# Convolution's and attention's output projections as seven block products, with the gated sum taken by DMA in DRAM

## The chip, the cores and the metric

One core of a Trainium2 chip runs the kernel in one launch. The metric is the device time of that launch in microseconds. Shown are three runs of the kernel before and one profiled execution, from which all rows come. In the profile PE is TensorE's matmuls and PEld its weight loads, DVE is VectorE, ACT ScalarE, POOL GpSimd and SP SyncE, which here only issues DMAs.

## The reference

The layer takes x of 1024 tokens by 1024 channels, all in float32. Three branches are computed from h = RMSNorm(x), each with an output projection of 1024 x 1024 and a gate per element:

```python
o = rms_norm(o, subln_g) * jnp.asarray(1.0 - lam_init, o.dtype)
y_attn = o.reshape(B, S, DIFF_WIDTH) @ w_attn_o
y_conv = short_gated_conv(conv_in, conv_w) @ w_conv_o
y_mem = memory_attention(q_m, mem_n, w_mem_kv, mq_norm_g, mk_norm_g) @ w_mem_o
g = jax.nn.sigmoid((gate_logits + b_gate).astype(jnp.float32))
merged = g[:, :, 0] * y_attn + g[:, :, 1] * y_conv + g[:, :, 2] * y_mem
x = x + merged @ w_o
x = x + jnp.square(jax.nn.relu(rms_norm(x, norm_mlp_g) @ w_mlp_in)) @ w_mlp_out
```

## The kernel before

Every large product is taken in float32r with both operands split in two: a high half (a ScalarE cast) and a low half (a subtraction, mostly on VectorE), and three matmuls, high x high, high x low and low x high, add up in PSUM. So 1024 channels of one 128 x 512 block are 8 x 3 = 24 matmuls of 512 columns.

There are two sets of buffers. In the old pool (tile pool and psum, lines 112 and 113) the kernel norms x, computes the memory branch and the attention heads, and fills PE's gaps with matmuls of a generator, `stream`: first convolution and gate projections (`fill_steps`), then the three output projections (`merge_steps`). What the branches gave lies in DRAM by channel: m_dram, c_dram, o_dram and the gate logits z_dram. `sum_jobs` (line 529) forms sums of MLP weight blocks DRAM to DRAM by DMAs on POOL's queue, one job in three stages of attention (line 833); they are needed since the MLP's two products are already done as seven block products instead of eight (a Winograd form of Strassen's scheme, `ORDER` at line 842).

The output projections run after the last head, PE in the order in which it is written out (`T.pin`), loads in the order in which SP is given them (`pin_load`). `prep(b)` loads and splits the whole operand of branch b into old-pool slots while the branch ahead of it ends; `branch_steps(b)` (line 571) goes over eight column blocks of 128 channels c and two halves of 512 tokens. Each has 24 matmuls. VectorE multiplies the PSUM result with the sigmoid of the gate (lines 589 and 591), POOL adds it to merged (line 592), and for the last branch POOL stores merged to mg_dram (line 594). Other engines' orders are set by a scheduler that works from priorities and its own idea of times.

Then the old pool is closed and the new one (`xp`, `bp`, line 862 on) begins. `load_m` and `load_wo` fetch merged and w_o, `wo_mm` multiplies eight token tiles, `wo_out` adds x, norms, and stores, and `up_steps` (line 1027) runs the up-projection's block products in the order of `seq1` (line 933): pairs (g, i) of column group g and product i. Products 1, 6, 7 and 4 add up in PSUM banks X, products 2, 5 and 3 in banks Z; after 1, 6 and 7 ScalarE copies X to a tile snap (line 1045), which the next product in the same X banks has to wait for. Tags give the numbers of buffers: "wraw" 4, "wop" 3, "sn" 3, "c" 7, "x" 14, "t" 4 halves.

Of the kernel before, what the change touches and what calls it, by code (L numbers as in the profile page):

```python
# [60 lines left out]
def tile_hybrid_block(ctx: ExitStack, tc: tile.TileContext, x, mem, norm_mix_g, norm_mem_g, w_in, b_gate,  # L61
# [483 lines left out]


    mg_dram = dram.tile([KT, P, S], F32, name="mg_dram")
    merged = [None] * KT

    srcs = {2: (w_mem_o, m_dram), 1: (w_conv_o, c_dram), 0: (w_attn_o, o_dram)}  # L550
    ready = {}
# [19 lines left out]
    def branch_steps(b):  # L571
        w_src = srcs[b][0]
        w, z = ready.pop(b)
        for c in range(KT):
            gt = rowt("gt")
            load(gt, z_dram[b, c])
            A.activation(gt, gt, AF.Sigmoid, bias=bg[:, b * KT + c:b * KT + c + 1])
            wn = load_w(w_src[:, (c + 1) * P:(c + 2) * P], P, "wh") if c + 1 < KT else None
            if b == 2:
                merged[c] = slot("merged", F32, tag="m")  # L580
            if c == KT - 1:
                if b:
# [18 lines left out]

    def load_head(h):
# [205 lines left out]
    for s in range(ns):  # L808
# [67 lines left out]
        return xp.tile([P, 1024 // n, n], F32, tag="wraw", bufs=4, name=name)  # L876

    def blk(name, tag):
        return xp.tile([P, 2, 512], F32, tag=tag, bufs={"sn": 3, "c": 7}[tag], name=name)

    def half_blk(name):
        return xp.tile([P, 512], F32, tag="t", bufs=4, name=name)

# [7 lines left out]
    tq = {t: half_blk("t2") for t in range(4, NT)}  # L891
    xr = {}

    def load_m(hf, kk):
# [23 lines left out]
    def wo_out(t, ps):  # L918
# [16 lines left out]
    for g in range(2, NG):  # L935
        seq1 += [(g, 6), (g, 5), (g, 7)]
        for i, last in ((1, 4), (2, 3)):
            if g < NG - 1:
                seq1.append((g + 1, i))
            seq1.append((g, last))  # L940
    R1, W1 = {}, {}

    def load1(n):
        if n < len(seq1):
            g, i = seq1[n]
            r = R1[n] = raw4("w1raw", 256)
            if i in (1, 2, 4):
                h, c = {1: (0, 0), 2: (1, 0), 4: (1, 1)}[i]
                load(r, w1v[h, c, g])
            else:  # L950
                load(r, sw1[{5: 0, 7: 1, 6: 2, 3: 3}[i]].rearrange("(k p) (g n) -> g p k n", p=P, n=256)[g])

    def split1(n):
        if n < len(seq1):
            t = W1[n] = wpair("w1", 256)
            split(t, R1.pop(n), V)


    X = {}
# [59 lines left out]
    def put_u(i, g, t):  # L1019
        G.dma_start(u_dram[i, g], t)  # L1020

    ps1 = {}

    def up(n):
        run(up_steps(n))

    def up_steps(n):

        g, i = seq1[n]
        key = "X" if i in (1, 6, 7, 4) else "Z"  # L1030
        if i in (1, 2, 5):
            ps1[g, key] = banks(key)
        ps = ps1[g, key]
        w = W1.pop(n)
        for j in range(2):
            for k in range(4):
                for q, (a, b) in enumerate(((0, 0), (0, 1), (1, 0))):
                    T.matmul(ps[:, j, :], lhsT=w[:, a, k, j * P:(j + 1) * P], rhs=X[i][b][:, k, :],
                             start=i in (1, 2, 5) and k == 0 and q == 0, stop=k == 3 and q == 2,
                             skip_group_check=True)  # L1040
                    if (12 * j + 3 * k + q) % 8 == 7 and k + j + q < 6:
                        yield
        if i in (1, 6, 7):
            s = B[g, "s", i] = blk("snap", "sn")
            A.copy(out=s, in_=ps)
        if i == 2:
            out1(g, "c11", ps, B.pop((g, "s", 1)))
            put_u(1, g, B[g, "c11"])
        if i == 7:
            out1(g, "c22", ps1[g, "Z"], B.pop((g, "s", 7)), -1)  # L1050
            put_u(4, g, B[g, "c22"])
        if i == 4:
            out1(g, "c21", ps, sign=-1)
# [1 line left out]
        if i == 3:  # L1055
            out1(g, "c12", ps, B.pop((g, "s", 6)))
            c11, c12, c21, c22 = (B.pop((g, c)) for c in ("c11", "c12", "c21", "c22"))

            sub(V, c22, c22, c12)
            sub(V, c12, c11, c12)  # L1060
            V.scalar_tensor_tensor(out=c11, in0=c22, scalar=-1.0, in1=c11, op0=ALU.mult, op1=ALU.subtract)
            V.scalar_tensor_tensor(out=c21, in0=c21, scalar=-1.0, in1=c11, op0=ALU.mult, op1=ALU.subtract)
            for k, t in ((5, c22), (7, c12), (6, c11), (3, c21)):
                put_u(k, g, t)

    load_m(0, 0)
    load_wo(0)
# [24 lines left out]
    for t in range(4, NT):  # L1092
        ps = banks("XZ"[t % 2])
        wo_mm(ps, t, range(KT), (0,))
        first_half(t - 4)
        wo_mm(ps, t, range(KT), (1,))
        wo_out(t, ps)
        second_sums(t)
        load1(t - 4)
        if t >= 6:  # L1100
            split1(t - 6)
    alloc_x(6, 5, 7, 4, 3)
    for n in range(len(seq1)):
        load1(n + 4)
        split1(n + 2)
        if n < 4:
            parts = second_half(4 + n)
            for _ in up_steps(n):
                run(parts, 1)
            run(parts)  # L1110
        else:
            up(n)


    w2v = w_mlp_out.rearrange("(h g j p) (d n) -> h d g p j n", h=2, j=2, p=P, d=2)
# [121 lines left out]
```

## Time and profile before

| | us |
|---|---|
| median of 3 runs | 2261.43 |
| lowest, highest | 2259.38, 2262.69 |
| profiled execution, its own time | 2260.93 |
| its span | 2259.2 |
| PE busy | 2200.5 |
| DVE, ACT, POOL busy | 1165.6, 943.8, 574.3 |

A matmul's busy time runs past the start of the next one, so the start-to-start distance is what a matmul costs in a row without gaps. A timeline row is start, busy time, engine, line, operation, out<-in, shape and, in brackets, the idle time before it and what ended that. A row of the windows is the window, its length, busy time and count of PE, PEld, DVE, ACT and POOL, PE's granted clock as a share of 2.4 GHz, the mean busy share of the 16 DMA engines and GB/s. A row of instruction groups is line, engine, operation, out<-in, shapes and count, then busy time in all, mean ns of one, and idle time before with its releasers.

### The profile page before, as it was taken

How to read it: one execution, taken by the hardware profiler on the slowest of the kernel's cores; microseconds unless marked ns; L12 is line 12 of the kernel's file. 1: busy time of each engine (PE TensorE's matmuls, PEld its weight loads, DVE VectorE, ACT ScalarE, POOL GpSimd, SP SyncE). 2: the span in 40 equal slices, each digit the busy share in tenths (PEclk: the TensorE clock that was granted, in tenths of full speed). 3: DMA queues.
4: the chain of work that ended last, by engine and by line, in shares of the span. 5: the costliest groups of instructions: out<-in, count | busy, mean ns of one | idle time of the engine just before them, and what ended most of it. 6: DMA issues, size and time to landing. Idle time of an engine off the chain costs nothing.

```text
span 2259.2 us, 30413 instructions
## 1 busy us (share of the span) xinstructions
PE 2200.5 (97%) x11280; PEld 1893.7 (84%) x11280; DVE 1165.6 (52%) x2127; ACT 943.8 (42%) x2134; POOL 574.3 (25%) x813
## 2 busy tenths in 40 slices
PE   6999999999999999999999999999999999999999
PEld 6999888888888888888888888877778888788887
DVE  6755455555555555555555333324446555754442
ACT  5544445444545454454545432312333222444331
POOL 5422223232333333232323223430401010000000
PEclk9999999999999999999999999999999999999999
DMA  6412246546554575561211544544336555865571
GB/s 198 133 59 64 88 158 157 124 147 168 143 156 145 117 166 144 160 147 43 84 43 71 162 159 135 169 162 169 121 104 213 182 202 185 305 261 186 199 267 57
DMA packets 225108, 336.11 MB, mean 149 GB/s; under 512 B 17216, under 2 KB 156480, under 8 KB 221632
## 3 DMA queue, kind: packets, MB, share of 16 engines
q1 hardware_dynamic: 183760, 203.98, 27.6%
q0 software_dynamic: 24320, 104.86, 16.6%
q10 hardware_dynamic: 16880, 25.33, 3.1%
q8 instruction: 89, 1.46, 0.3%
q14 instruction: 59, 0.48, 0.1%
HBM read 267.02 MB, written 134.22 MB: 178 GB/s over the span
## 4 chain that ended last, share of the span: by engine, by line
PE 89%; DVE 4%; DMA 3%; ACT 2%; issue 2%; POOL 0%; SPq 0%; ACTq 0%; DVEq 0%; POOLq 0%
PE ps_mm L89 42%; PE X L89 16%; PE Z L89 13%; PE ps_sc L89 11%; PE ps_tr L89 3%; PE ps_tr L93 3%; DVE wlo L186 1%; PE Z L93 1%; DMA rawh<-in_w_in_dram 0%; DVE ql L666 0%; ACT qh L661 0%; DMA w2raw<-in_w_mlp_out_dram 0%; DMA mraw<-mg_dram 0%; DMA xt<-in_x_dram 0%; DVE whl L186 0%
## 5 line engine op out<-in xcount | busy, mean ns | idle before, releaser
L89 PE MATMUL ps_mm<-hT,whi 128*128 128x512 f32 x1536 | 490.8, 400 | 0.7 <-DVE vst L636 0.7
L89 PEld LDWEIGHTS ps_mm<-hT,whi 128*128 128x128 f32 x1536 | 279.7, 189 | 51.0 <-DVE vst L636 2.5
L89 PE MATMUL ps_mm<-hT,wlo 128*128 128x512 f32 x768 | 301.9, 393 | 0.0
L89 PE MATMUL ps_mm<-whh,hT 128*128 128x384 f32 x1024 | 276.7, 341 | 2.2 <-DVE inner L477 1.9
L186 POOL TENSOR_TENSOR wlo<-raw,whi 128x512 fp32r<-128x512 f32 (+2 forms) x120 | 139.1, 1164 | 214.0 <-ACT whi L204 186.5
L89 PEld LDWEIGHTS ps_mm<-whh,hT 128*128 128x128 f32 x1024 | 186.4, 188 | 7.9 <-DVE inner L477 3.7
L89 PE MATMUL X<-w,u 128*128 128x512 f32 x768 | 174.9, 389 | 1.3 <-ACT snap L1185 1.3
L89 PE MATMUL ps_mm<-whl,hT 128*128 128x384 f32 x512 | 172.0, 336 | 2.5 <-DVE whl L186 1.8
L89 PEld LDWEIGHTS X<-w,u 128*128 128x128 f32 x768 | 144.1, 188 | 31.6 <-ACT snap L1185 1.7
L89 PEld LDWEIGHTS ps_mm<-hT,wlo 128*128 128x128 f32 x768 | 144.9, 189 | 27.6
L204 ACT CAST whi<-raw 128x512 fp32r<-128x512 f32 (+2 forms) x240 | 117.8, 537 | 66.7 <-PE ps_sc L89 22.0
L638 POOL TENSOR_TENSOR sq<-qk 128x256 f32<-128x256 f32 x64 | 41.8, 654 | 382.0 <-ACT qk L633 382.0
L186 DVE TENSOR_TENSOR wlo<-raw,whi 128x512 fp32r<-128x512 f32 (+2 forms) x120 | 102.4, 857 | 68.9 <-ACT whi L204 68.2
L176 POOL TENSOR_TENSOR r<-r,mhalf 128x1 f32<-128x1 f32 (+1 forms) x186 | 133.1, 715 | 15.3
L89 PE MATMUL Z<-w,u 128*128 128x512 f32 x576 | 131.6, 389 | 1.6 <-DVE snap L854 1.6
L89 PEld LDWEIGHTS Z<-w,u 128*128 128x128 f32 x576 | 108.0, 188 | 24.7 <-DVE snap L854 2.4
L89 PE MATMUL ps_mm<-x,whi 128*128 128x512 f32 x384 | 119.1, 391 | 0.0
L89 PE MATMUL ps_sc<-x,whi 128*128 128x512 f32 x384 | 118.3, 389 | 0.0
L175 POOL TENSOR_SCALAR r<-ss 128x1 f32<-128x1 f32 (+1 forms) x186 | 37.3, 201 | 287.2 <-ACT ps_tr L732 131.4
L691 ACT ACTIVATE e<-ps_sc,negm 128x256 f32<-128x256 f32 (+7 forms) x128 | 94.1, 740 | 31.6 <-DVE negm L688 31.6
L1020 POOL DMA_DIRECT2D u_dram<-c x56 | 29.9, 535 | 300.7 <-DVE c L1016 148.9
L89 PE MATMUL ps_mm<-whi,hT 128*128 128x256 f32 x512 | 102.9, 292 | 0.0
(238 smaller groups left out, 4552.4 us busy)
## 6 DMA issues: line engine op xcount, KB each, us to landing
raw<-in_w_in_dram SPq DMA_DIRECT2D x56, 512.0 KB, 3.9
u_dram<-c POOLq DMA_DIRECT2D x56, 512.0 KB, 3.7
uraw<-u_dram SPq DMA_DIRECT2D x56, 512.0 KB, 6.3
sw<-in_w_mlp_in_dram POOLq DMA_DIRECT2D x6, 4096.0 KB, 24.6
sw<-in_w_mlp_out_dram POOLq DMA_DIRECT2D x6, 4096.0 KB, 28.6
w1raw<-sw SPq DMA_DIRECT2D x32, 512.0 KB, 3.3
w2raw<-sw SPq DMA_DIRECT2D x32, 512.0 KB, 4.5
rawh<-in_w_in_dram SPq DMA_DIRECT2D x64, 192.0 KB, 2.8
```

The source lines that it names most:

```text
L89: return cls.pin(nc.tensor.matmul(*a, **kw))
L93: return cls.pin(nc.tensor.transpose(*a, **kw))
L175: G.tensor_scalar(r, ss, 1.0 / n, EPS, op0=ALU.mult, op1=ALU.add)
L176: last_norm[0] = G.tensor_tensor(out=r, in0=r, in1=mhalf[:, 0:width], op=ALU.pow)
L186: eng.tensor_tensor(out=lo, in0=raw, in1=f(hi), op=ALU.subtract)
L204: A.copy(out=hi[:, a:b, :], in_=raw[:, k0 + a:k0 + b, :])
L638: G.tensor_tensor(out=sq, in0=qk, in1=qk, op=ALU.mult)
L691: A.activation(e[:, 0:n], sc[:, 0:n], AF.Exp, scale=-1.0, bias=negm[:, c:c + 1], accum_out=sums[:, c:c + 1])
L1020: G.dma_start(u_dram[i, g], t)
```

## The change

The memory branch stays where it was. It gates its result and stores it to mg_dram from ScalarE's queue. The other two projections leave the old pool. They become 2 x 14 block products of 24 matmuls in the new pool, ahead of w_o: two column groups of 256 and seven products, with the weights' sums formed in DRAM beforehand by 16 further jobs (1 MB each), and the operand's sums by VectorE. Each of the eight results of a branch (256 channels by 512 tokens) is gated and added to mg_dram by a DMA on POOL's queue with `accum_op=add`. The class Stage takes the place of load1, split1 and up_steps, for both the branches and the up-projection. Besides, the up-projection's last two groups get another order, and its first loads and splits are written ahead of wo_out.

```diff
+    sbr = {b: [dram.tile([512, 512], F32, name=f"sb{b}{i}") for i in range(4)] for b in (1, 0)}
...
+        todo = [([w[h * 512:(h + 1) * 512, c * 512:(c + 1) * 512] for c in range(2) for h in range(2)], sbr[n])
+                for n, w in ((1, w_conv_o), (0, w_attn_o))]
+        for (q, t, r, s), z in todo + [(a, sw1), ((b[0], b[2], b[1], b[3]), sw2)]:
...
-            if c == KT - 1:
-                if b:
-                    prep(b - 1)
...
-                if b == 2:
-                    V.tensor_tensor(out=merged[c][:, sl], in0=ps, in1=gt[:, sl], op=ALU.mult)
-                else:
-                    V.tensor_tensor(out=gt[:, sl], in0=ps, in1=gt[:, sl], op=ALU.mult)
-                    G.tensor_tensor(out=merged[c][:, sl], in0=merged[c][:, sl], in1=gt[:, sl], op=ALU.add)
-                if b == 0:
-                    G.dma_start(mg_dram[c][:, sl], merged[c][:, sl])
+                V.tensor_tensor(out=gt[:, sl], in0=ps, in1=gt[:, sl], op=ALU.mult)
+                store(mg_dram[c][:, sl], gt[:, sl])
...
-        for b in (2, 1, 0):
-            yield from branch_steps(b)
+        yield from branch_steps(2)
...
-        if s % 3 == 1:
+        if 2 <= s < 18 or s % 3 == 0:
             run(jobs, 1)
...
+    one = [(0, 1), (0, 2), (1, 1), (1, 2), (0, 6), (0, 5), (0, 7), (1, 6), (0, 4), (1, 5), (1, 7), (0, 3), (1, 4),
+           (1, 3)]
...
+    def gate(g, i):
+        b, gg = g
+        ch, th = {2: (0, 0), 7: (1, 1), 4: (1, 0), 3: (0, 1)}[i]
+        c = 4 * ch + 2 * gg
+        t = gates[g, i] = blk("gt", "t")
+        load(t, z_dram[b, c:c + 2, :, th * 512:(th + 1) * 512].rearrange("c p n -> p c n"))
+        for j in range(2):
+            A.activation(t[:, j], t[:, j], AF.Sigmoid, bias=bg[:, b * KT + c + j:b * KT + c + j + 1])
+        return c, th
+
+    def done_br(g, i, ps, s):
+        if i in (1, 6, 7):
+            t = snaps[g, i] = blk("snap", "sn")
+            A.copy(out=t, in_=ps)
+        if i in (2, 7, 4, 3):
+            c, th = gate(g, i)
+            z = gates.pop((g, i))
+            if i == 4:
+                src = ps
+            else:
+                src = snaps.pop((g, {2: 1, 7: 7, 3: 6}[i]))
+                add(V, src, s.ps[g, "Z"], src)
+
+            V.scalar_tensor_tensor(out=z, in0=src, scalar=-1.0 if i in (7, 4) else 1.0, in1=z, op0=ALU.mult,
+                                   op1=ALU.mult)
+            G.dma_start(mg_dram[c:c + 2, :, th * 512:(th + 1) * 512].rearrange("c p n -> p c n"), z,
+                        accum_op=ALU.add)
...
+    for n in range(len(seq_br)):
+        q, m = divmod(n, len(one))
+        br.load(n + 4)
+        br.split(n + 2)
+        if q == 0 and m < 4:
+            run(prep, 1)
+        if q + 1 < len(BR) and m == 4:
+            nxt = chain(first_br(BR[q + 1]), second_br(BR[q + 1]))
+        run(br.steps(n))
+        if m in (5, 6, 10, 11, 13):
+            run(nxt, 1)
...
+    g, h = NG - 2, NG - 1
+    seq1 += [(g, 6), (g, 5), (g, 7), (h, 1), (g, 4), (h, 2), (h, 6), (h, 5), (h, 7), (g, 3), (h, 4), (h, 3)]
...
+        up.load(t - 4)
+        if t >= 6:
+            up.split(t - 6)
         wo_out(t, ps)
         second_sums(t)
-        load1(t - 4)
-        if t >= 6:
-            split1(t - 6)
```

`Stage.load(n)` loads the weight block of product n (512 KB), `split(n)` makes its halves and `steps(n)` gives PE its 24 matmuls. `first_br(b)` loads four operand blocks of branch b (`block`: 256 channels by 512 tokens) and splits them for products 1 and 2 (`put_br`: one instruction on ScalarE and one on VectorE); `second_br(b)` loads twelve more, forms the sums and splits those of products 6, 5, 7, 4 and 3. Gate tiles have the tag "t", which now has two buffers.

The first place is ScalarE's order where the work goes from the old pool to the new. Before (raw tiles of merged and w_o are mraw and woraw):

```order
L577 ACTIVATE gt<-gt,bg 128x1024
L204 CAST whi<-raw 128x384 x2
L204 CAST whi<-raw 128x256
L577 ACTIVATE gt<-gt,bg 128x1024
L860 CAST mT_15527<-mraw 128x1024
L860 CAST wo_15507<-woraw 128x1024
L860 CAST wo_15508<-woraw 128x1024
```

And in the changed kernel (wraw is a product's weight block, xb1 and xb2 are operands of products 1 and 2):

```order
L579 ACTIVATE gt<-gt,bg 128x1024
L101 DMA mg_dram<-gt 128x512 x6
L851 CAST w<-wraw 128x1024 x2
L968 CAST xb1h<-raw 128x1024 x2
L851 CAST w<-wraw 128x1024
L968 CAST xb2h<-raw 128x1024 x2
L940 COPY snap<-X 128x1024
```

Six stores of the memory branch stand there now, then two weight casts, and the casts of merged and w_o have moved behind the two branches.

The second place is SP's order around the loads of merged. Before:

```order
L98 DMA gt<-z_dram 128x1024
L98 DMA raw<-in_w_attn_o_dram 128x8x128
L98 DMA gt<-z_dram 128x1024
L98 DMA mraw<-mg_dram 128x2x512
L98 DMA woraw<-in_w_o_dram 128x1024 x2
L98 DMA mraw<-mg_dram 128x2x512
```

And in the changed kernel (sb_105 is one of the four sums of the attention projection's weights):

```order
L98 DMA wraw<-in_w_attn_o_dram 128x4x256
L98 DMA gt<-z_dram 128x2x512
L98 DMA wraw<-sb_105 128x4x256
L98 DMA gt<-z_dram 128x2x512 x4
L98 DMA mraw<-mg_dram 128x2x512
L98 DMA woraw<-in_w_o_dram 128x1024 x2
L98 DMA mraw<-mg_dram 128x2x512
```

Four gate loads stand in a row ahead of the first mraw, where one stood.

The third place is PE's order near the end of the up-projection, in its last column group. Before, product 7 ends and product 4 begins in the same banks X:

```order
L89 MATMUL X<-x7h,w_18014 128x512 x2
L89 MATMUL X<-x7l,w_18014 128x512
L89 MATMUL X<-x7h,w_18014 128x512
L89 MATMUL X<-x4h,w_18043 128x512
L89 MATMUL X<-x4l,w_18043 128x512
```

In the changed kernel:

```order
L89 MATMUL X<-x7h,w 128x512 x2
L89 MATMUL X<-x7l,w 128x512
L89 MATMUL X<-x7h,w 128x512
L89 MATMUL Z<-x3h,w 128x512
L89 MATMUL Z<-x3l,w 128x512
```

The 24 matmuls of product 3 of the group before now stand between product 7 and product 4.

## Rows read from the trace of the kernel before

**Rows 1.** The page: busy time by engine, and the chain's shares.
```profile
PE 2200.5 (97%) x11280; PEld 1893.7 (84%) x11280; DVE 1165.6 (52%) x2127; ACT 943.8 (42%) x2134; POOL 574.3 (25%) x813
...
PE 89%; DVE 4%; DMA 3%; ACT 2%; issue 2%; POOL 0%; SPq 0%; ACTq 0%; DVEq 0%; POOLq 0%
```

**Rows 2.** The chain by time, last two of 32 units: start, us, what.
```profile
1500.74 5.44 PE ps_mm L89 x24
1506.18 5.45 PE ps_sc L89 x24
```

**Rows 3.** Windows, in the two branches and in the up-projection.
```profile
1700.00:1900.00 200.00, 200.00 (x884) 165.68 (x883) 117.94 (x100) 57.84 (x58) 20.79 (x39) 1.00 0.57 197
1345.00:1500.00 155.00, 155.00 (x686) 128.38 (x685) 47.05 (x66) 42.76 (x72) 66.39 (x64) 1.00 0.43 138
```

**Rows 4.** Timeline where the first pool ends.
```profile
1511.23 0.39 PE L89 MATMUL ps_sc<-x,wlo 128*128 128x512 f32 x1
1511.66 0.69 DVE L591 TENSOR_TENSOR gt<-ps_sc,gt 128x512 f32<-128x512 f32 x1 [4.68 <-PE ps_sc L89]
1512.13 0.49 PE L89 MATMUL X<-wo,mT 128*128 128x512 f32 x1 [0.51 <-ACT wo L860]
...
1515.74 2.50 PE L89 MATMUL X<-wo,mT 128*128 128x512 f32 x5 [3.11 <-DVE wo L854]
...
1520.60 1.93 PE L89 MATMUL X<-wo,mT 128*128 128x512 f32 x6
...
1522.36 1.52 PE L89 MATMUL Z<-wo,mT 128*128 128x512 f32 x6
```

**Rows 5.** Instruction groups of the up-projection, 1700 to 1900 us.
```profile
L854 DVE TENSOR_TENSOR w<-w1raw,w 128x1024 fp32r<-128x1024 f32 x37 | 45.1, 1219 | 24.3 <-ACT w L860 24.3
L860 ACT CAST w<-w1raw 128x1024 fp32r<-128x1024 f32 x37 | 38.9, 1052 | 61.0 <-PE Z L89 61.0
L857 DVE TENSOR_TENSOR c<-Z,snap 128x1024 f32<-128x1024 f32 x17 | 20.8, 1224 | 43.8 <-PE Z L89 22.9 <-ACT snap L1045 20.9
L1020 POOL DMA_DIRECT2D u_dram<-c x39 | 20.8, 533 | 177.1 <-DVE c L1016 73.2 <-DVE c L854 47.9 <-DVE c L1013 38.7
```

**Rows 6.** Timeline: a store issued by ScalarE; two VectorE instructions back to back.
```profile
1200.58 0.33 ACTq L101 DMA_DIRECT2D z_dram<-z  x1
...
1641.28 1.22 DVE L854 TENSOR_TENSOR w<-w1raw,w 128x1024 fp32r<-128x1024 f32 x1
1642.41 1.21 DVE L1016 SCALAR_TENSOR_TENSOR c<-c 128x1024 f32<-128x1024 f32 x1
```

**Rows 7.** DMA issues: count, KB each, median us from issue to landing.
```profile
u_dram<-c POOLq DMA_DIRECT2D x56, 512.0 KB, 3.7
...
gt<-z_dram SPq DMA_DIRECT2D x24, 512.0 KB, 4.0
...
rawx<-c_dram SPq DMA_DIRECT2D x8, 512.0 KB, 3.7
...
mraw<-mg_dram SPq DMA_DIRECT2D x8, 512.0 KB, 6.9
```

**Rows 8.** DMA in 270:310 (copying job), 413:455 (adding job), 416:441 (its queue).
```profile
sw<-in_w_mlp_in_dram POOLq DMA_DIRECT2D x1, 4096.0 KB, 16.5
...
sw<-in_w_mlp_in_dram POOLq DMA_DIRECT2D x1, 4096.0 KB, 26.0
...
q0 software_dynamic: 512, 4.06, 79.1%
```

**Rows 9.** DMA queue, packets, MB, share (1700:1900, 1950:2000), and windows.
```profile
q1 hardware_dynamic: 19008, 18.88, 29.7%
...
q1 hardware_dynamic: 4952, 12.27, 66.1%
...
1920.00:1940.00 20.00, 18.04 (x79) 14.59 (x79) 16.34 (x14) 7.79 (x9) 2.67 (x5) 1.00 0.82 284
1950.00:2000.00 50.00, 50.00 (x222) 41.41 (x221) 33.15 (x26) 22.90 (x23) 6.95 (x6) 1.00 0.77 288
```

**Rows 10.** Windows in attention with the sum jobs and after them.
```profile
250.00:1000.00 750.00, 743.10 (x3914) 650.44 (x3913) 413.42 (x1005) 366.01 (x1006) 248.31 (x362) 1.00 0.54 145
1000.00:1150.00 150.00, 148.99 (x787) 130.34 (x786) 81.46 (x207) 72.81 (x206) 44.20 (x67) 1.00 0.29 76
```

**Rows 11.** PE's waits, 1900 to 1960 us: total, times, longest.
```profile
PE X L89 <- ACT snap L1045: 2.0, 1, 2.0
```

More of the change, by code (lines that the diff above doesn't have):

```diff
@@ new lines, in tile_hybrid_block, with src_br @@
+    BR = (1, 0)
+    w_br = {1: w_conv_o, 0: w_attn_o}
+    in_br = {1: c_dram, 0: o_dram}
+    one = [(0, 1), (0, 2), (1, 1), (1, 2), (0, 6), (0, 5), (0, 7), (1, 6), (0, 4), (1, 5), (1, 7), (0, 3), (1, 4),
+           (1, 3)]
+    XB = {b: {i: [x8(f"xb{i}{c}", (4, 512)) for c in "hl"] for i in ORDER} for b in BR}
+    gates, snaps = {}, {}
+    def src_br(g, i):
+        b, g = g
+        if i in (1, 2, 4):
+            h, c = {1: (0, 0), 2: (1, 0), 4: (1, 1)}[i]
+            w = w_br[b][h * 512:(h + 1) * 512, c * 512:(c + 1) * 512]
+        else:
+            w = sbr[b][{5: 0, 7: 1, 6: 2, 3: 3}[i]]
+        return w.rearrange("(k p) (g n) -> g p k n", p=P, n=256)[g]
@@ new lines, in block, with put_br @@
+    def block(b, kk, h, th):
+        t = blk("raw", "c")
+        k = 4 * h + 2 * kk
+        load(t, in_br[b][k:k + 2, :, th * 512:(th + 1) * 512].rearrange("k p n -> p k n"))
+        return t
+    def put_br(b, i, kk, src):
+        hi, lo = (z[:, 2 * kk:2 * kk + 2, :] for z in XB[b][i])
+        if i in (4, 5):
+            A.activation(hi, src, AF.Copy, scale=-1.0)
+            V.scalar_tensor_tensor(out=lo, in0=src, scalar=-1.0, in1=f(hi), op0=ALU.mult, op1=ALU.subtract)
+        else:
+            A.copy(out=hi, in_=src)
+            sub(V, lo, src, f(hi))
@@ new lines, in first_br, with second_br @@
+    def first_br(b):
+        for h, i in ((0, 1), (1, 2)):
+            for kk in range(2):
+                put_br(b, i, kk, block(b, kk, h, 0))
+            yield
+    def second_br(b):
+        n2 = {}
+        for kk in range(2):
+            b12, b11, b22 = block(b, kk, 0, 1), block(b, kk, 0, 0), block(b, kk, 1, 1)
+            sub(V, b11, b12, b11)
+            n2[kk] = blk("n2", "c")
+            sub(V, n2[kk], b11, b22)
+            put_br(b, 6, kk, n2[kk])
+            put_br(b, 5, kk, b11)
+            yield
+        for kk in range(2):
+            b12, b22 = block(b, kk, 0, 1), block(b, kk, 1, 1)
+            sub(V, b12, b22, b12)
+            put_br(b, 7, kk, b12)
+            b21 = block(b, kk, 1, 0)
+            add(V, b21, b21, n2[kk])
+            put_br(b, 4, kk, b21)
+            put_br(b, 3, kk, b22)
+            yield
@@ new lines, in tile_hybrid_block @@
+    seq_br = [((b, g), i) for b in BR for g, i in one]
+    br = Stage(seq_br, src_br, lambda g: XB[g[0]], done_br)
+    prep = chain(first_br(BR[0]), second_br(BR[0]))
+    br.load(0)
+    br.load(1)
+    run(prep, 1)
+    br.split(0)
+    br.load(2)
+    br.load(3)
+    run(prep, 1)
+    br.split(1)
+    nxt = iter(())
+    for n in range(len(seq_br)):
[3 more added lines that the diff above has]
+        if q == 0 and m < 4:
+            run(prep, 1)
+        if q + 1 < len(BR) and m == 4:
[3 more added lines that the diff above has]
+            run(nxt, 1)
@@ L886, in tile_hybrid_block @@
+    run(nxt)
     wo_op = [x8(f"wo{k}", (2, 1024)) for k in range(KT)]
@@ L890, in tile_hybrid_block @@
     m_op[0] = [x8("mT0", (2, 2, 512)) for _ in range(4)]
-    tq = {t: half_blk("t2") for t in range(4, NT)}
+    tq = {}
+    for t in range(4, NT, 2):
+        z = blk("t2", "t")
+        tq[t], tq[t + 1] = z[:, 0], z[:, 1]
     xr = {}
@@ L934, in tile_hybrid_block, with src1 @@
             (1, 4), (2, 2), (1, 3)]
[L935 to L956, printed above, removed]
+    for g in range(2, NG - 2):
+        seq1 += [(g, i) for i in (6, 5, 7)] + [(g + 1, 1), (g, 4), (g + 1, 2), (g, 3)]
+    g, h = NG - 2, NG - 1
+    seq1 += [(g, 6), (g, 5), (g, 7), (h, 1), (g, 4), (h, 2), (h, 6), (h, 5), (h, 7), (g, 3), (h, 4), (h, 3)]
+    def src1(g, i):
+        if i in (1, 2, 4):
+            h, c = {1: (0, 0), 2: (1, 0), 4: (1, 1)}[i]
+            return w1v[h, c, g]
+        return sw1[{5: 0, 7: 1, 6: 2, 3: 3}[i]].rearrange("(k p) (g n) -> g p k n", p=P, n=256)[g]
     X = {}
@@ L1020, in put_u, with done1 @@
         G.dma_start(u_dram[i, g], t)
[L1022 to L1042, printed above, removed]
+    def done1(g, i, ps, s):
         if i in (1, 6, 7):
-            s = B[g, "s", i] = blk("snap", "sn")
-            A.copy(out=s, in_=ps)
+            t = B[g, "s", i] = blk("snap", "sn")
+            A.copy(out=t, in_=ps)
         if i == 2:
```

49 lines of the change are left out of this document (36 added, 13 removed).

## The prediction

> **What bounds the kernel now.** I read the page's first part and its chain, then the windows, then the places where the chain leaves TensorE. TensorE is busy for 97% of the span and the chain that ended last is 89% PE [rows 1], so a matmul taken out of a stretch without gaps comes off the end. The two branches that change are such a stretch: one half column block, 24 matmuls, takes 5.44 us of the chain [rows 2], which is 227 ns a matmul, and in 1345 to 1500 us PE is busy for 155.00 of 155 us at granted clock 1.00 while VectorE has 47.05 us and ScalarE 42.76 us [rows 3]. Where the work passes from the first pool of buffers to the second there is a gap [rows 4]: the last branch matmul starts at 1511.23 and frees the array at 1511.46, the second one of the output projection waits until 1515.74, and the next 17 run slowly until 1522.36. Eighteen matmuls take 10.9 us where 18 x 0.227 = 4.1 would do: 6.8 us are lost there today.
>
> **A. The products.** Each of the two branches had 16 units of 24 matmuls and gets 14. 32 - 28 = 4 units x 5.44 = **-21.8 us**, all of it on the chain [rows 2]. The launch has 96 matmuls fewer.
>
> **B. A second hand-over.** Today convolution and attention follow the memory branch inside the old pool without a gap. Afterwards the memory branch ends the old pool, and the first product starts in the new one. I count from the end of the last memory matmul. VectorE's gate multiply takes 0.69 us [rows 4], and the order shows that ScalarE issues the last of six stores (0.33 us [rows 6]) before it touches the new phase: 1.05 us. Then ScalarE casts w of product 0, w of product 1 and the first half of the operand, three times 1.05 us [rows 5]: 4.2. VectorE follows with the low halves in that order. It starts on the first at 2.1, and back to back such instructions start 1.13 us apart [rows 6], so the third is done at 2.1 + 2 x 1.13 + 1.22 = 5.6. The second matmul needs it. The loads are not what ends last: they wait for PE's 8th matmul of 24 in the last unit, so they are issued 3.6 to 2.8 us before time zero and land, at 3.7 us each as the convolution's rows do today [rows 7], by 1. Idle is about 5.5 us. After today's shorter idle 17 matmuls took 1522.36 - 1515.74 = 6.6 us instead of 3.9 [rows 4], so I add 2.8 for the clock. **+8.3 us**; from 6.8 (today's hand-over again) to 12 (the loads land as late as today's 6.9 us mraw rows [rows 7], and ScalarE waits for them).
>
> **C. The hand-over to the output projection.** In SP's order of the new kernel the last four gate loads stand in a row just ahead of mraw and woraw. A gate tile has two buffers, so the load for the last gate waits until the sum of the gate two before it has landed in DRAM. How long an adding DMA of 512 KB takes from SBUF, no row shows. Plain stores of that size land in 3.7 us [rows 7]; among the 4 MB jobs an adding one took 26.0 us and a copying one 16.5 [rows 8]. I scale: 3.7 x 26.0 / 16.5 = 5.8, with 3.7 and 26.0 as ends. Let T be the end of the product two before the last. VectorE adds and multiplies (T+2.4), POOL issues (0.53 [rows 5], T+2.9), the sum lands (T+8.7), the gate load lands 4.0 later [rows 7] (T+13.0 with its issue), two sigmoids of half width end at T+14.1. ScalarE's casts of mraw and woraw stand behind them, VectorE's multiply and three halves too: the projection's second matmul can go at T+17.5. PE is done with its products at T+10.9. 6.6 us idle and 2.8 for the clock are 9.4, against 6.8 today: **+2.6 us**, from 0 (plain-store speed) to +22 (26.0).
> The store row is 3.7 us. The Trainium skill, "DMA: Bandwidth & Descriptors" (Anatomy of one DMA, SWDGE path), gives such a DMA about 2.0 us plus bytes over 436 GB/s, an estimate of 3.2 us here, with no extra for adding; by it C would be 0 and the sum 2.6 us lower. The 4 MB rows speak against it: the formula gives 11.6 us for both, the trace 16.5 and 26.0 [rows 8].
>
> **D. VectorE in the first branch.** Per branch VectorE gets 14 weight halves, 14 operand halves, 8 sums of blocks, 6 additions from PSUM and 8 gate products: 50 instructions of 1.22 us [rows 5], paced at 1.13 [rows 6]: 57 us of PE's 76. On average it is covered. At the start it is not far ahead: laying its order out at that pace from B, the low half of the 7th product's operand is ready about 0.4 us after PE asks for it, that of the 5th just in time. **+1 us**, from 0 to +4. ScalarE has 34 full-width casts and copies (1.05 us) and 16 half-width sigmoids, about 45 us of 76: covered.
>
> **E. Transfers.** Per branch there are 14 weight blocks, 16 operand blocks (each half is read twice), 8 gates and 8 sums, 46 transfers of 512 KB in 76 us. The trace prices them as shares of 16 engines: 1 KB rows 18.88 MB in 29.7% of 200 us, 1.65 us each; 2 and 4 KB rows 12.27 MB in 66.1% of 50 us, 1.41 us each [rows 9]; adding jobs 4.06 MB in 79.1% of 25 us, 2.55 us for 512 KB [rows 8]. 14 x 1.65 + 24 x 1.41 + 8 x 2.55 = 77 us a branch, as long as PE's work. Today's branches ask for about half of that (share 0.43 [rows 3]). Weight blocks are issued about four products ahead, 20 us, which covers a landing time of 9 us or so; but with so little room some blocks will come late. **+3 us**, from 0 to +27 (rival 2).
>
> **F. Sixteen more sums in attention.** They go into POOL's queue behind a norm each, spaced by one stage, and the 4 MB ones move later by up to 16 stages. Nothing but POOL's next norm stands behind them. In 250 to 1000 us, with all 16 of today's jobs, PE lacks 6.9 us of 750, in 1000 to 1150 without any 1.0 of 150 [rows 10]: 1.4 against 1.0 per 150 us, about 0.1 us per job, so +2 at most for 16 full-size ones, which these are not. ScalarE and VectorE also get another order of the weight halves there. **+1 us**, from -1 to +4.
>
> **G. The end of the up-projection.** Today the last column's seventh product is followed at once by the fourth in the same PSUM banks, and PE waits 2.0 us for ScalarE's copy, the longest wait of that stretch [rows 11]. In the new order the sixth column's third product stands between. **-2.0 us**, from -2.5 to 0. The weight split that is now issued before wo_out moves nothing in VectorE's order at that place, so I count nothing for it.
>
> The memory branch's stores move to ScalarE's queue: 16 x 0.33 us over 87 us, with ScalarE under a third busy [rows 3]. POOL loses 32 additions that nothing waits for any more.
>
> **Sum.** -21.8 + 8.3 + 2.6 + 1 + 3 + 1 - 2.0 = -7.9. The profiled execution took 2260.9 us (span 2259.2), 0.5 under the median of 2261.4. 2260.9 - 7.9 = **2253**.
>
> **The rivals.**
> 1. Clean hand-overs, chance 0.22. Both cost what today's costs, since the ready queues ahead are as full, and transfers stay hidden: -21.8 + 6.8 + 0 + 0 + 0 + 0 - 2.0 = -17, 2244 us. For it: weights are loaded four ahead, operands of attention come during convolution. Against it: six stores and two weight casts stand ahead of the first operand.
> 2. The transfers bound the two branches, slower, chance 0.15. 2 x 77 = 154 us of transfers at the highest share that a 20 us stretch reaches today, 0.82 in 1920 to 1940, where PE was not full either [rows 9], are 188 us; PE with B and D needs 162. +26 in place of E's 3 gives -7.9 - 3 + 26 = +15, 2276 us. It decides from a share of about 0.89 downwards (154 / 0.89 = 173, the 11 us that A to G without E leave). For it: the sum of the shares. Against it: 50 us at a mean of 0.77 with PE full [rows 9].
> The Trainium skill, same page (Issuing engines are not separate DMA queues), says that DMAs from SP, ScalarE and GpSimd run on the same 16 engines and interleave; by that rule three queues bring no bandwidth and rival 2 stands. Today's shares never exceed 1 in a stretch with all three, which agrees but is no test.
> 3. The gate chain, no change, chance 0.18. Four gates in a row at a branch's end need one gate per product. The loop of two gates is sum + 0.53 + 0.3 + 4.0 + 1.1 + 1.2 us; at 5.8 it takes 13 us against 10.9 of PE. If an adding DMA takes 12 us, C rises by 6.2, and in the first branch VectorE's weight half for the product three after stands behind the late gate multiply: some 3 us more. -7.9 + 9.2 = +1.3, 2262 us. For it: the factor of 1.6 between adding and copying jobs. Against it: 512 KB from SBUF is short.
>
> **How the numbers follow.** My own sum has 0.42, with 2248 to 2258 for itself; 0.03 is left for what I have not seen. A change under 0.2% (4.5 us, about what a measurement of this kernel can tell from none) is 2256.4 to 2265.4. Faster: 0.22 + 0.38 = 0.60. Same: 0.04 from my own, 0.18, 0.02: 0.24. Slower: 0.16. The range runs from rival 1 past rival 3: 2244 to 2266, which leaves out most of rival 2 and a little below.
>
> **What the profile after would show.** A: 672 matmuls named X or Z from the xb operands, about 5.44 us per 24 in the chain. B: 5 to 6 us of PE idle before the first xb1l, ended by VectorE, then slow matmuls. C: gate loads waited for by ScalarE just before mT, PE idle 6 to 7 us. D: a wait of PE for xb7l under 2 us. E: DMA share near 0.9 there; waits of PE for weight halves would speak for rival 2. F: PE idle before 1200 us within 3 us of today's. G: no wait of X for snap before the last up-projection product. I am wrong if PE's idle time in the two branches is above 15 us, or if the gain is under 4.

## The result and the profile after

The changed kernel took 2294.0 us (median of 4 runs, 2293.7 to 2297.1) against 2262.1 for the kernel before (4 runs beside it): a ratio of 1.0143, with a 95% interval of 1.0131 to 1.0155. It is slower, by 32 us; forecast was 2253, with a range that ended at 2266. The profiled execution took 2293.9 us (span 2292.1), 32.9 us more of span than before, and the accounts below are made against that.

PE is busy for 10.6 us less than before [rows 1], and yet the span grew. The page of the changed kernel, first part and DMA queues (packets, MB, share of 16 engines):

```profile
PE 2189.9 (96%) x11184; PEld 1881.2 (82%) x11184; DVE 1216.7 (53%) x2139; ACT 975.8 (43%) x2138; POOL 531.7 (23%) x773
...
q1 hardware_dynamic: 190352, 218.66, 29.2%
q0 software_dynamic: 32832, 125.84, 21.7%
```

**Attention.** ScalarE copies 48 gate blocks z out of PSUM during attention. The rows of that copy, one for each kernel (duration in ns, then first and last start in us), date its end. Before:

```profile
L502 ACT COPY z<-ps_mm x48: 580/588/599, 305.0 to 1247.5; 128x512 f32<-128x512 f32 x48
```

Changed:

```profile
L503 ACT COPY z<-ps_mm x48: 579/588/599, 307.5 to 1270.5; 128x512 f32<-128x512 f32 x48
```

From first to last that is 942.5 us before and 963.0 after: 20.5 us are lost inside attention, where no product of the two branches is yet made. The waits of PE up to 1200 us in the changed kernel (total, times, longest):

```profile
PE ps_mm L89 <- ACT z L503: 17.4, 2, 9.7
PE ps_tr L93 <- DVE memt L278: 9.0, 1, 9.0
PE ps_tr L93 <- DVE e L691: 4.9, 6, 3.7
```

Before, the first row was 0.3 us in all, and the longest wait of the third 1.6. Three waits make the difference: 7.6 us at 619, 3.7 at 864, 9.7 at 1012. How the last one comes about stands in four views of the changed kernel. POOL issues an adding 4 MB job:

```profile
980.38 1.93 POOL L533 DMA_DIRECT2D sw<-in_w_mlp_out_dram  x1
```

SP is loading the next head's weights (the eight loads span 41.4 us here, 28.8 to 39.9 before):

```profile
962.14 41.36 SPq L98 DMA_DIRECT2D rawh<-in_w_in_dram  x8
```

ScalarE's casts wait for them, and the copy z that frees PE's bank stands behind these casts (start, us, idle before it and what ended it):

```profile
1000.98 0.51 ACT L603 CAST whh<-rawh 128x384 fp32r<-128x384 f32 x1 [2.24 <-DMA rawh<-in_w_in_dram]
1005.79 0.51 ACT L603 CAST whh<-rawh 128x384 fp32r<-128x384 f32 x1 [4.30 <-DMA rawh<-in_w_in_dram]
1006.21 1.13 ACT L204 CAST whi<-raw 128x512 fp32r<-128x512 f32 x2
1010.61 0.51 ACT L603 CAST whh<-rawh 128x384 fp32r<-128x384 f32 x1 [3.27 <-DMA rawh<-in_w_in_dram]
1011.14 0.59 ACT L503 COPY z<-ps_mm 128x512 f32<-128x512 f32 x1
```

The DMA view of 990 to 1016 us shows what the loads met: a landing time of 10.3 us, where the page's median is 3.2 (2.8 before), and POOL's queue with more than two thirds of the engines:

```profile
q0 software_dynamic: 1646, 3.34, 69.0%
...
rawh<-in_w_in_dram SPq DMA_DIRECT2D x2, 192.0 KB, 10.3
```

A head's loads recur every 126 us (442 to 482, 570 to 599, 696 to 724, 821 to 861, 947 to 978 us before). The eight adding jobs of the kernel before stand at 370, 413, 511, 606, 749, 792, 889 and 986 us: each is over, or not yet begun, when such a run of loads starts or ends (the one of 792 us lands 2.4 us into a run); only copying jobs fall into one. Shifted by the 16 new jobs, three adding ones (590, 834 and 980 us) fell into the runs of 571 to 618, 832 to 864 and 962 to 1003 us. Copying jobs slow the loads too: in the runs of 442 and 821 us before, one load took 13 and 14 us to land, and PE waited 1.5 us at most. Beside the adding jobs of 590 and 980 us the longest took 21 and 23 us.

**The two branches.** From the first product's start to the last one's end 177.9 us pass; 28 x 5.44 [rows 2] are 152.3. Windows of 20 us there (as in [rows 3]):

```profile
1400.00:1420.00 20.00, 19.47 (x86) 15.78 (x85) 18.24 (x17) 15.42 (x17) 2.39 (x2) 1.00 1.06 332
1460.00:1480.00 20.00, 18.29 (x75) 13.88 (x76) 14.99 (x14) 10.27 (x12) 2.96 (x3) 1.00 1.05 311
1480.00:1500.00 20.00, 9.30 (x34) 6.99 (x33) 10.75 (x10) 9.45 (x11) 1.85 (x2) 0.75 0.87 251
1520.00:1540.00 20.00, 20.00 (x90) 16.58 (x89) 7.08 (x6) 5.28 (x7) 2.41 (x2) 1.00 0.46 86
```

The DMA share is at 1, PE is nearly full beside it for a while, and then it stands for half of 1480 to 1500. After the two long waits its matmuls run slowly (granted clock 0.50 in 1491 to 1502 us, which is 1.2 GHz). PE's timeline names what it lacks, the operand of the second branch's seventh product:

```profile
1491.52 0.80 PE L89 MATMUL X<-xb7h,w 128*128 128x512 f32 x1 [5.22 <-ACT xb7h L968]
...
1497.80 0.80 PE L89 MATMUL X<-xb7l,w 128*128 128x512 f32 x1 [5.48 <-DVE xb7l L845]
```

Its three loads are the last row of SP's timeline here. Ahead of them stand gate loads, which wait for a buffer:

```profile
1457.29 0.36 SPq L98 DMA_DIRECT2D gt<-z_dram  x1
1457.71 1.49 SPq L98 DMA_DIRECT2D raw<-o_dram  x3
1459.29 1.32 SPq L98 DMA_DIRECT2D wraw<-sb  x2
1469.98 0.36 SPq L98 DMA_DIRECT2D gt<-z_dram  x1
1470.43 0.97 SPq L98 DMA_DIRECT2D wraw<-sb  x2
1473.84 0.36 SPq L98 DMA_DIRECT2D gt<-z_dram  x1
1474.31 0.41 SPq L98 DMA_DIRECT2D wraw<-in_w_attn_o_dram  x1
1477.93 0.36 SPq L98 DMA_DIRECT2D wraw<-sb  x1
1478.34 1.53 SPq L98 DMA_DIRECT2D raw<-o_dram  x3
```

The gap of 9.4 us before 1469.98 ends as the sum that POOL issued at 1460.36 lands. SP's own waits from 1360 to 1545 us say how much of its time goes that way, 91.6 us in 13 waits:

```profile
SPq L98 <- DMA mg_dram<-gt: 91.6, 13, 15.8
SPq L98 <- DVE w L845: 29.1, 7, 7.1
```

**The hand-over to the output projection.** PE's timeline there, against [rows 4]:

```profile
1542.38 0.39 PE L89 MATMUL Z<-xb3h,w 128*128 128x512 f32 x1
1552.86 0.80 PE L89 MATMUL X<-wo,mT 128*128 128x512 f32 x1 [10.08 <-ACT wo L851]
1554.12 2.50 PE L89 MATMUL X<-wo,mT 128*128 128x512 f32 x5 [0.47 <-DVE wo L845]
```

### The profile page after: what moved, and what is told of

Its sections match the earlier page's. It is cut to its first block, busy times and chain, and to the rows that moved or that the text cites. A ratio compares the mean times of both kernels' runs of the same rounds, so it can differ in the third digit from the quotient of the medians.

```text
span 2292.1 us, 30234 instructions
## 1 busy us (share of the span) xinstructions
PE 2189.9 (96%) x11184; PEld 1881.2 (82%) x11184; DVE 1216.7 (53%) x2139; ACT 975.8 (43%) x2138; POOL 531.7 (23%) x773
## 5 line engine op out<-in xcount | busy, mean ns | idle before, releaser
L186 POOL TENSOR_TENSOR wlo<-raw,whi 128x512 fp32r<-128x512 f32 (+2 forms) x96 | 116.4, 1217 | 148.5 <-ACT whi L204 147.9
L851 ACT CAST w<-wraw 128x1024 fp32r<-128x1024 f32 x84 | 88.0, 1050 | 115.2 <-PE Z L89 75.1
L845 DVE TENSOR_TENSOR w<-wraw,w 128x1024 fp32r<-128x1024 f32 x84 | 102.6, 1223 | 62.6 <-ACT w L851 62.6
L204 ACT CAST whi<-raw 128x512 fp32r<-128x512 f32 (+2 forms) x192 | 96.7, 552 | 38.4 <-PE ps_mm L89 10.1
L845 DVE TENSOR_TENSOR u<-uraw,u 128x1024 fp32r<-128x1024 f32 x56 | 73.3, 1308 | 59.3 <-ACT u L851 58.9
L679 DVE CUSTOM_DVE_ANT_0 ps_sc<-ps_sc,mask 128x256 f32<-128x256 f32 (+7 forms) x128 | 95.1, 779 | 14.0 <-PE ps_sc L89 12.4
```

The source lines that it names most:

```text
L186: eng.tensor_tensor(out=lo, in0=raw, in1=f(hi), op=ALU.subtract)
L204: A.copy(out=hi[:, a:b, :], in_=raw[:, k0 + a:k0 + b, :])
L679: V.tensor_tensor_reduce(out=sc[:, 0:n], in0=sc[:, 0:n], in1=mask[:, S - n:S], scale=-1.0, scalar=BIG, op0=ALU.add, op1=ALU.min, accum_out ...
L845: eng.tensor_tensor(out=out, in0=a, in1=b, op=ALU.subtract)
L851: A.copy(out=hl[:, 0], in_=raw)
```

## The experiments

Theory J puts attention's loss on three large adding jobs (4 MB each) that meet a head's loads; its rival J2 puts it on the 16 new small jobs (1 MB). Theory Q puts the branches' loss on gate loads that hold SP's queue until a sum has landed, T on the transfers themselves, and P (formed after the second group of runs) on the place of the last operand loads in the queue. Eleven kernels ran. The table has the median, the ratio to the kernel before as measured beside it (2261.8 to 2263.7 us) with its interval, and three stretches of the one profiled execution: z (first to last copy z), branches (start of the first xb1h matmul to that of the last xb3h one; 152.1 without a gap) and hand-over (from there, in the kernel before from its last branch matmul, to the first Z of the output projection; 1.6 without a gap). From one execution to the next such a stretch moves by 2 or 3 us: the four kernels with e6's placement (e6, e8, e10, e11) have z from 943.7 to 946.2.

| kernel | us | ratio (95%) | z | branches | hand-over |
|---|---|---|---|---|---|
| before | 2262.1 | | 942.5 | | 6.8 |
| changed | 2294.0 | 1.0143 (1.0131 to 1.0155) | 963.0 | 177.7 | 14.0 |
| e1 large jobs late, in the kernel before | 2286.4 | 1.0108 (1.0089 to 1.0128) | 965.3 | | |
| e2 large jobs at their old places | 2282.0 | 1.0086 (1.0067 to 1.0106) | 952.6 | 177.2 | 12.4 |
| e3 three gates | 2284.1 | 1.0097 (1.0076 to 1.0119) | 964.0 | 167.6 | 14.5 |
| e4 half weights | 2284.6 | 1.0102 (1.0080 to 1.0124) | 963.1 | 168.9 | 14.0 |
| e5 plain stores | 2277.8 | 1.0076 (1.0060 to 1.0091) | 962.8 | 166.8 | 10.3 |
| e6 all jobs placed | 2276.2 | 1.0064 (1.0047 to 1.0082) | 946.2 | 176.2 | 14.7 |
| e7 free gates | 2284.2 | 1.0095 (1.0071 to 1.0118) | 961.7 | 175.9 | 1.6 |
| e8 = e3 + e6 + e7 | 2258.8 | 0.9987 (0.9976 to 0.9998) | 945.4 | 169.3 | 1.6 |
| e9 early operand | 2285.5 | 1.0099 (1.0083 to 1.0116) | 965.0 | 164.9 | 16.1 |
| e10 = e8 + e9 | 2253.8 | 0.9962 (0.9948 to 0.9977) | 943.7 | 165.7 | 1.6 |
| e11 = e10 + e4 | 2249.6 | 0.9942 (0.9927 to 0.9957) | 945.4 | 167.0 | 1.6 |

**e1.** The kernel before, its 16 large jobs issued at the changed kernel's stages.

```diff
-        if s % 3 == 1:
+        if s == 17 or s >= 18 and s % 3 == 0:
             run(jobs, 1)
```

> The kernel before with its 16 large sum jobs put at the stages at which the changed kernel issues them (17, 18, 21, 24, ..., 60), and nothing else changed. Theory J (an adding 4 MB job that is under way when SP loads the next head's weights holds those loads up, and the changed kernel moved three such jobs, at stages 21, 36 and 45, onto these loads): PE waits of 3 to 10 us for ScalarE's z or VectorE's e three times between 600 and 1020 us, attention ends 18 to 22 us later, 2279 to 2284 us. Rival J2 (the 16 additional small jobs and their bytes cost the time, not the place of the large ones): no small job is here, so 2260 to 2264 us. My prediction's step F (moving costs nothing, POOL has room): 2260 to 2264 us.

It lost 22.7 us (2286.4 against 2263.7 for the kernel before, measured beside it); J's upper end was 2284. No small job and no product is in it, and its waits of PE from 230 to 1200 us are the changed kernel's:

```profile
PE ps_mm L89 <- ACT z L502: 16.8, 2, 9.0
PE ps_tr L93 <- DVE e L700: 5.8, 6, 3.6
```

J is shown: the place of the large jobs alone makes the loss. J2 and step F fall.

**e2.** The changed kernel, large jobs at their old stages, a small one a stage after each.

```diff
-        if 2 <= s < 18 or s % 3 == 0:
+        if s % 3 == 1:
             run(jobs, 1)
+        elif s % 3 == 2:
+            run(jobs2, 1)
```

> The changed kernel with its large sum jobs back at the stages of the kernel before (every third, from 1), the 16 small ones one stage after each. Theory J: attention's three stalls go, 20 us less, 2272 to 2276 us. Rival J2 (the additional jobs cost it wherever they are): 2290 to 2296 us.

A miss: 12 us less, not 20. Between J and J2, so it decides nothing alone. Around 812 us a small adding job follows a large one issued at 797, and the small one, which lands at 835, reaches into the loads that begin at 826 there; from 800 to 850 us PE is busy for 46.1 of 50 us (50.0 before). e6 tells the two apart.

**e6.** As e2, with the small jobs away from the loads and from the large adding ones.

```diff
+    SMALL = (0, 2, 6, 15, 26, 30, 39, 49, 50, 55, 56, 57, 58, 59, 60, 61)
...
+        elif s in SMALL:
+            run(jobs2, 1)
```

> The changed kernel with the large sum jobs at the stages of the kernel before and the small ones at stages at which neither a head's weights are loaded nor a large adding job is under way. Theory J (it is the overlap with the head's loads that costs): attention as long as before, 20 to 23 us less, 2270 to 2275 us; the 10 us that remained when the small jobs stood one stage behind the large ones go too. Rival J2 (the bytes of the small jobs cost it): 2280 to 2284 us, as there.

17.9 us less than the changed kernel, 1 short of J's band and 4 from J2's. Attention takes 946.2 us from first to last z, 16.8 less than changed and 3.7 more than before. All 32 jobs are there, and e10 has 943.7 with the same placement; so their bytes cost 1 to 4 us, and the overlap the rest.

**e3.** One gate buffer more; it later holds g2_row.

```diff
-... bufs={"sn": 3, "c": 7, "t": 2}[tag] ...
+... bufs={"sn": 3, "c": 7, "t": 3}[tag] ...
-    g2_row = xp.tile([P, S], F32, tag="g2", bufs=1, name="g2_row")
+    g2_row = blk("g2_row", "t").rearrange("p h n -> p (h n)")
```

> The changed kernel with three gate buffers instead of two (the third later holds g2_row, so that no room is added). Bytes and jobs stay. Theory Q (a gate load waits in SP's queue until the sum of the gate two before has landed, and weight and operand loads stand behind it): SP is hardly held, PE's idle time in the two branches falls from 21 to under 9 us and the hand-over to the output projection by 3 to 6, 2274 to 2282 us. Rival T (the transfers themselves bound the two branches, 156 us of them at full share): the waits stay or move to other loads, 2289 to 2296 us.

9.9 us less, 2 past Q's band, and all of it in the branches (177.7 to 167.6). SP's waits for sums fall from 91.6 us to

```profile
SPq L98 <- DMA mg_dram<-gt: 50.8, 8, 15.9
```

The hand-over did not gain, against what Q expected: the last gate still waits for a sum.

**e4.** Half of each weight block's bytes; the other half of the block is left out, the loaded half is used twice.

```diff
-                load(r, self.src(*self.seq[n]))
...
+                    load(r[:, 0:2], w[:, 0:2])
+                    r = self.raw[n] = r[:, 0:2].unsqueeze(1).broadcast_to([P, 2, 2, 256])
```

> The changed kernel with only the first half of each weight block of the two branches loaded and used twice, which leaves out the other half: 28 x 256 KB fewer, everything else as it is. Theory Q: the gate loads wait for the same sums, which land a little sooner; gain 0 to 6 us, 2288 to 2294 us. Rival T: about 28 x 0.8 = 23 us of transfers fewer, and the waits in the two branches go: 2272 to 2280 us.

9.4 us less: more than Q allowed, less than T wanted. The branches take 168.9 us, nearly as with three gates. So neither theory holds alone. PE's waits at the second branch's seventh product fall from 10.7 us in all to 4.8 in e3 and 4.2 here; most of what is left is for a copy of X that stands on ScalarE behind a cast of the late operand.

**e5.** Plain stores for the adding DMAs (the sum over the branches is left out).

```diff
-                        accum_op=ALU.add)
```

> The changed kernel with plain stores in place of the 16 adding DMAs, which leaves out the sum over the branches. An adding DMA landed 6 to 8 us after its issue in the trace of the changed kernel. Theory Q+T (the gate load waits for a landing that is long because it adds and shares the engines): the landing falls to about 4 us, the gate loads go out earlier, PE's idle time in the two branches falls from 21 to under 10 us and the hand-over by 3 to 5: 2275 to 2281 us. If the adding is not what makes the landing long (only the shared engines): 2288 to 2295 us.

16.2 us less, within Q+T's band: 10.9 in the branches, 3.7 in the hand-over. The landing fell too, though from 6 to 10 us, not 6 to 8, and not as far as 4. The DMA views of 1375 to 1525 us price the adding (queue: packets, MB, share; issues: count, size, median us to landing). Changed kernel:

```profile
q0 software_dynamic: 3264, 6.29, 25.5%
...
mg_dram<-gt POOLq DMA_DIRECT2D x12, 512.0 KB, 8.7
```

Plain stores:

```profile
q0 software_dynamic: 1872, 6.82, 11.5%
...
mg_dram<-gt POOLq DMA_DIRECT2D x14, 512.0 KB, 6.2
```

Near the end of the second branch the engines have room. Changed kernel in 1509 to 1540 us (share 0.56), then plain stores in 1497 to 1524 (0.33):

```profile
mg_dram<-gt POOLq DMA_DIRECT2D x4, 512.0 KB, 6.1
...
mg_dram<-gt POOLq DMA_DIRECT2D x4, 512.0 KB, 3.3
```

**e7.** The second branch's gates in the buffers of the operand blocks, which are free by then.

```diff
-        t = gates[g, i] = blk("gt", "t")
+        t = gates[g, i] = blk("gt", "t" if b else "c")
```

> The changed kernel with the gates of the second branch in the seven buffers of the operand blocks, which that branch no longer fills; no room, no byte and no instruction more. Theory Q: no gate load of the second branch waits for a sum, the four last gates are there in time, and the hand-over to the output projection loses 3 to 5 us instead of 13; in the second branch the waits for xb7 fall: together 14 to 20 us less, 2274 to 2280 us. Rival T (bytes): the waits for xb7 stay, only the hand-over gains: 2284 to 2289 us.

9.8 us less, T's line rather than Q's: the hand-over gained 12.4, the branches 1.8. SP's waits from 1360 to 1545 us show what became of Q there:

```profile
SPq L98 <- DMA mg_dram<-gt: 53.2, 7, 13.1
SPq L98 <- DVE w L845: 49.4, 13, 8.9
...
1478.26 2.10 SPq L98 DMA_DIRECT2D raw<-o_dram  x3
```

The hold by sums fell as far as in e3, and between 1457 and 1480 us there was none (18.3 us in the changed kernel). Yet the three loads for product 7 left at 1478.3 as before: SP waited for weight buffers instead, and PE still waited 5.2 and 2.7 us for xb7 (5.2 and 5.5 in the changed kernel). Without the gates' hold these loads were just as late.

With free gates the output projection follows the last product without a gap. PE's timeline of e10, which has the same edit:

```profile
1511.29 0.39 PE L89 MATMUL Z<-xb3h,w 128*128 128x512 f32 x1
1511.52 1.52 PE L89 MATMUL X<-wo,mT 128*128 128x512 f32 x6
```

That is better than the kernel before, which loses 6.8 us at that place. The hand-over's loss was the gate chain; what is left of it is a wait for VectorE's last sum, three groups of matmuls later (2.1 us in e7, 0.7 in e10).

**e8.** e3, e6 and e7 together.

> The changed kernel with the jobs placed as in e6, three gate buffers and the second branch's gates in the operand buffers. If J and Q are the whole cause, what is left of the change is 96 matmuls fewer (-21.8), the first hand-over (+8), some waits in the branches (+3 to +6), the end of the up-projection (-2): 2249 to 2256 us, faster than both kernels. If the transfers bound the branches beyond that: 2260 to 2268 us.

2258.8 us: between the two bands, 0.13% faster than the kernel before, which its interval only just tells from none. The branches still take 169.3 us. Its longest wait there was 4.8 us for a copy that ScalarE had queued behind a cast of the late operand, hence P.

**e9.** The changed kernel with the last quarter of the second branch's operands prepared four products earlier.

```diff
-        if m in (5, 6, 10, 11, 13):
+        if m in (5, 6, 10, 11, 13) or q and m == 1:
             run(nxt, 1)
```

> The changed kernel with one step of the preparation written earlier: the last quarter of the second branch's operands (three loads, xb7, xb4, xb3) after that branch's second product instead of its sixth, so that the three loads stand further ahead in SP's queue. Theory P (those loads are issued late because of where they stand, and the two longest PE waits of the branches, 5.2 and 5.5 us for xb7, are theirs): these two waits go with the slow matmuls behind them, 8 to 14 us less, 2280 to 2286 us. Theory Q alone (SP is held by gate loads, the place in the queue is second): a gain under 4 us, 2290 to 2294 us, since the loads then wait behind the gate loads that stand ahead of them.

8.5 us less, at P's upper end: the branches fall by 12.8 us to 164.9, the shortest of all. In 1250 to 1575 us the waits for xb7 are down to one row:

```profile
PE X L89 <- DVE xb7l L845: 0.2, 1, 0.2
```

P is shown for these two waits: bytes, buffers and the adding are as before, and SP is held by sums nearly as long (87.8 us). The three loads now leave 17.7 us after the branch's first matmul; it was 32.0 in the changed kernel, 31.8 in e7 and 28.2 in e3. Against that stand a new wait of 3.3 us for a weight cast, at the branch's fourth product, and a hand-over 2 us longer.

**e10.** e8 with the edit of e9: all four.

> Kernel e8 (jobs placed, three gates, free gates) with this earlier step as well. Theory P: the waits for snap (4.8) and xb7l (2.0) of e8, both behind the late loads, go: 5 to 9 us under e8's 2258.8, that is 2250 to 2254 us, faster than the kernel before by 0.4 to 0.6%. Rival T (no room in the transfers, the loads push others back): 2256 to 2260 us.

2253.8 us (6 runs, 2248.1 to 2258.4), within P's band, ratio 0.9962 (0.9948 to 0.9977): faster than both kernels, than the one before by 0.4%. Attention is back at 943.7 us and the hand-over has no gap.

**e11.** e10 with e4's edit (half of each weight block left out).

> Kernel e10 with only the first half of each weight block of the two branches loaded and used twice, which leaves out the other half (28 x 256 KB). Rival T (what is left in the branches is the transfers): 5 to 10 us under e10. If the rest is VectorE and ScalarE (step D, their order): within 3 us of e10.

2249.6 us, 4.2 under e10, with intervals that overlap; between the expectations, and the profiled branches are no shorter (167.0 against 165.7). It shows only that halving the weights' bytes does not bring back the 10 us that the branches of e10 still lose beyond 152.1 and the first hand-over's slow start.

## Why the prediction was wrong, step by step

The spans differ by +32.9 us; the steps as measured, from rows of the two profiled executions (rounded, they add up to 33.0):

| step | forecast | measured | from |
|---|---|---|---|
| A products | -21.8 | -21.8 | 96 matmuls fewer, units of 5.44 us |
| B second hand-over | +8.3 | +7.9 | first 24 matmuls 13.3 us instead of 5.44 |
| C output projection | +2.6 | +6.6 | first 18 matmuls 17.5 us against 10.9 |
| D and E branches | +4 | +22.0 | the other 27 units 168.9 us instead of 146.9 |
| F jobs in attention | +1 | +20.5 | copies z, first to last |
| G up-projection | -2.0 | -2.5 | from the projection's last Z to the end |
| not forecast | 0 | +0.3 | start +2.5, rest of the output projection -2.2 |

**A, B and G** held in mechanism and size. In B the wait was 4.2 us for ScalarE's xb1h and 0.8 for VectorE's xb1l, then slow matmuls. G's wait for snap [rows 11] is gone. The 2.5 us at the start are there in the profile of e1 as well (first z at 307.3), which is the kernel before up to stage 1: they belong to the execution, not to the change.

**F is the step that failed worst**, with +20.5 us for +1; E is the other. "Nothing but POOL's next norm stands behind them" looked along POOL's queue and not along the engines that its jobs share with SP's loads. And the 0.1 us per job was an average over places that all happened to be harmless [rows 10]. The kernel before held the warning: the adding job's 79.1% of all engines for 25 us [rows 8] and head loads every 126 us. The Trainium skill, "DMA: Bandwidth & Descriptors" (Issuing engines are not separate DMA queues), says that DMAs of SP, ScalarE and GpSimd run on the same 16 engines and interleave; the trace agrees, with a head's load at 10.3 us instead of 3.2 beside a job. I had applied that to the branches only.

**E and D.** D held: in the first branch PE waited 0.5 us for xb7l. E failed, and in the second branch: its 14 units took 96.3 us instead of 76.2, which is 20 of the 22 us. The sum of the shares was right: 154 us forecast, 156 measured (86.9% of the 180 us from 1364 to 1544). What I made of it was not. "Weight blocks are issued about four products ahead, 20 us, which covers a landing time of 9 us or so" gave the weight blocks a lead and did not ask what lead the operand loads have. The last three of these left 8 us before PE asked for the seventh product's second half (1478.3 against 1486.3), and the one that it waits for took 10.2 us to land. At a share of 1 the operand loads of that branch landed in 8.6 us (median) instead of 3.7 [rows 7].

I had also taken SP for free to issue, when gate loads held it for 91.6 us. I had seen the gate loads ahead of mraw (step C), and not the same loads ahead of everything else. But the hold is not what decides: e7 shortens it and keeps 7.9 of the 10.7 us of waits, e9 keeps it and loses them. The place in the queue is shown to be enough; a shorter hold (e3) and fewer bytes (e4) took away more than half of the waits.

Rival 2 had the size, +26 in place of 3, but as a bound by throughput it falls: e9 and e10 move all the bytes and lose 12 us less. Its rate was a misreading: 0.82 is not the highest share of 20 us in the kernel before. Two windows there are above 1 with PE full, so the remark that shares never exceed 1 falls too:

```profile
800.00:820.00 20.00, 20.00 (x109) 17.51 (x108) 10.00 (x25) 8.96 (x25) 5.90 (x11) 1.00 1.11 225
1960.00:1980.00 20.00, 20.00 (x90) 16.57 (x89) 12.76 (x11) 8.43 (x8) 0.00 (x0) 1.00 1.04 401
```

A share of 1 is no fixed rate either: 225 GB/s in one of these, 401 in the other. e10 keeps PE busy for 95% of 140 us in its branches at a mean share of 0.99:

```profile
1360.00:1500.00 140.00, 133.53 (x582) 108.67 (x581) 99.90 (x87) 81.89 (x95) 14.53 (x12) 1.00 0.99 296
```

**C and rival 3** named the mechanism, and the size was off. Idle was 10.1 us, not 6.6. The estimate of 5.8 us for an adding DMA was close (6.0 and 6.2 for the last two of the chain). But the sum that the last gate load waited for left POOL 1.7 us later than forecast, since VectorE was still at the gate before it, and that gate load took 5.6 us and not 4.0. e7 takes the chain away.

The formula in the Trainium skill, "DMA: Bandwidth & Descriptors" (Anatomy of one DMA, SWDGE path), gave 3.2 us, with nothing extra for adding. The trace agrees for plain stores where the engines have room (3.3 us in e5, at a share of 0.33); it does not for adding ones (6.1 us at 0.56), nor for either in 1375 to 1525 us with the engines nearly full (6.2 and 8.7 us). In engine time, 11.5% of 150 us for 6.82 MB against 25.5% for 6.29 MB is 1.3 and 3.2 us of all engines per 512 KB.

Rival 2's 2276 with F's 20 us would have been 2296. No rival had a loss in attention, and the range left out most of rival 2: it was too narrow at the side that the sum of the shares spoke for.

**What stays open.** e10's branches still lose about 10 us beyond the first hand-over, in waits for ScalarE's copies and VectorE's weight halves of 0.4 to 2.5 us each and slow matmuls after them. Halving the weights' bytes did not give it back (e11); whether a better order on ScalarE would was not tried. Why e3 brings the operand loads 4 us forward and e7 does not, at the same hold of SP in all, was not tested either: e3 also frees the first branch's gates.

## What to carry to other kernels

Work that runs on spare DMA time had no price per job here: its price was which loads it overlapped. Before moving such jobs, lay their busy windows over the periodic loads of the stretch. When a load waits for a buffer that only an outgoing DMA frees, ask which loads stand behind it in the same queue, and price landings at the share they will meet, not at the median of a quiet stretch. A held queue looks like the cause; see by an experiment whether the late load would have left sooner without the hold, or has to be written earlier.

## What the runs showed beyond that

An adding DMA into DRAM cost 2.4 times the engine time of a plain store of the same size (3.2 against 1.3 us per 512 KB, e5), and with room on the engines it landed in 6.1 us against 3.3. With the share near 1, 512 KB loads that land in 3.7 to 4.0 us elsewhere took 9 to 10 us (median in e10's branches: 9.6 for gates, 10.0 for the second branch's operands). Issued early enough, they still left PE, after the first hand-over, with no wait above 0.4 us put down to an operand's cast or low half.
